# Parts of sums kept in DRAM instead of being built twice, in a float32 block of convolution and gated linear attention

## The chip, the cores and the metric

The kernel runs on one core of a Trainium2 chip (trn2). The metric is the time of one execution on the device in microseconds (us); the time of a kernel is the median of its runs. Beside it a profile of one execution shows what each engine did: TensorE (PE for matmuls, PEld for loading the stationary operand), VectorE (DVE), ScalarE (ACT), GpSimd (POOL) and SyncE (SP), which here does nothing but issue DMAs, in order.

## What is computed

One layer on 512 tokens of 2048 features, in float32. A combined projection feeds two branches, a short gated convolution and a chunked gated linear attention (GLA):

```python
h = rms_norm(x, norm_g)
ch, cb, cc, cz, gq, gk, gv, gr, gd = split(h @ w_in)      # 1024 x4, 512, 512, 1024, 1024, 16 columns
y_conv = cb * conv3(cc * ch) * silu(cz)                   # causal, three taps, per column
glog   = log_sigmoid(gd @ w_up + b_gate) / 16             # 8 chunks of 64 tokens
state  = exp(sum(glog over chunk)) * state + k_dec.T @ gv # per chunk, 4 heads
y_gla  = head_norm(gq @ state) * silu(gr)
out    = rms_norm(x + concat(y_conv, y_gla) @ w_out, final_g)
```

## The kernel before

**Numbers.** Each float32 operand is split into a high part (a cast to the matmul's own float32 form, on ScalarE) and a low part (the difference, on VectorE), and each product is three matmuls: high by high, low by high and high by low. `split_small` (lines 146 to 151) splits a tile of 128x512, `split` (124 to 126) one of 128x1024.

**Units with seven products.** The value columns, the four convolution groups and part of the output are done by `st_unit` (641 to 722): each of its five units before the output, named UV, 0, 1, 2 and 3, replaces the eight block products of a 2x2 split of both operands by seven, of 48 matmuls each. For this it needs sums of quarters of the activations, called s1, s2, s3 and s4: `sums` (552 to 566) makes four tiles of 128x512 for each of four pairs `j`, with one VectorE operation each (line 559). s4, s1 and s2 are then split into two parts each; s3 is kept whole, and `place_third` (598 to 601) splits it into the place of the second half of tokens of the normed activations `hT`. Sums of quarters of the weights are made on VectorE while the unit runs (line 687).

**The same sums, twice.** `quarter_sums(j)` (578 to 582) loads two 512 KB blocks of `xT` (tiles `raw_qx`), scales each half on ScalarE (line 574), makes the sums and splits them. It runs once for each `j` between the four `q_head` calls, for UV. During UV `restore_quarter` puts the normal second half of `hT` back for the eight `r_block` calls that come next, between which the steps of GLA run. The parts of the sums are given up after UV, because GLA needs the buffers. After `r_block(6)` come `quarter_sums(0)` and `(1)`, after `r_block(7)` `(2)` and `(3)`, a second time, for units 0 to 3; `place_third` then runs again.

**Order of the program.** The engines' and queues' orders are laid out ahead of time by a list planner that takes program order as priority and lets an instruction go early when its data and buffers are there. Buffers come from pools: `k2` has 44 tiles of 128x512, among them all parts of the sums; `raw` has 8 blocks of 128x1024 for loaded weights, for `raw_qx` and for the rows that go into `y_raw`; the high and low parts of weights have 4 blocks each. All loads and stores but ten stand on SP's queue. Eight of the ten are the copies of the chunk decays, 2 KB each, which ScalarE issues; four small transposes (`dp`, line 366) read them on TensorE.

**Already kept in DRAM.** `keep` is a pool in DRAM. `r_block` stores its result as `r_raw` (line 528), and `gated_rows` loads it back at the end of unit 0, multiplies it by `oT` and stores it as `y_raw` (lines 506 to 512).

Of the kernel before, what the change touches and what calls it, by code (L numbers as in the profile page):

```python
# [8 lines left out]
F32 = mybir.dt.float32  # L9
# [4 lines left out]
P = 128  # L14
D = 2048
S = 512
# [30 lines left out]
SPLITBUFS = 4  # L47
STC = 4
UV = 5
HT = S // 2  # L50


@with_exitstack
def hybrid_block(ctx: ExitStack, tc: tile.TileContext, xT, x, params, w_tm, w_ft, w_st, w_up, b_gate, w_out, final_g, out):
    nc = tc.nc
# [6 lines left out]
    keep = ctx.enter_context(tc.tile_pool(name="keep", bufs=1, space=bass.MemoryType.DRAM))  # L62
# [3 lines left out]
    def t2(name):  # L66
        return k2.tile([P, S], F32, tag="k2", name=name)

    def t2r(name):
        return k2.tile([P, S], F32R, tag="k2", name=name)  # L70
# [23 lines left out]
    for _ in range(WARM):  # L94
# [9 lines left out]
        out=trif[:, 0:P], in_=trif[:, 0:P], compare_op=ALU.is_gt, fill=0.0, base=0, pattern=[[-1, P]],  # L104
# [29 lines left out]
    def load_raw(src, n, name):  # L134
        raw = raw_tile(name)
        return raw, nc.sync.dma_start(out=raw[:, 0:n], in_=src)
# [9 lines left out]
    def split_small(t, name):  # L146
        hi = t2r(f"{name}_hi")
        lo = t2r(f"{name}_lo")
        nc.scalar.copy(out=hi, in_=t)
        nc.vector.tensor_sub(out=lo, in0=t, in1=hi.bitcast(F32))  # L150
        return hi, lo
# [11 lines left out]
    def load_x(kt):  # L163
        c, i = divmod(kt, HPC)
        if kt == 0:
            r = x_first
            nc.scalar.activation(hT_hi[c][:, i, 0:HT], r[:, 0:HT], AF.Copy, scale=g_in[:, 0:1])
            nc.vector.tensor_scalar(
                out=hT_hi[c][:, i, HT:S], in0=r[:, HT:S], scalar1=g_in[:, 0:1], scalar2=None, op0=ALU.mult
            )  # L170
# [120 lines left out]
    for tt in range(TT):  # L291
        nc.vector.tensor_scalar(
            out=dg[:, tt * P : (tt + 1) * P], in0=ident, scalar1=rstd[:, tt : tt + 1], scalar2=None, op0=ALU.mult
# [85 lines left out]
    def chunk_splits(tt):  # L379
        kv_split[tt] = [split_small(kv[tt][j], f"kv{tt}_{j}") for j in range(3)]  # L380
# [142 lines left out]
    def r_block(b):  # L523
        r = ft_unit(HEADS + b, b == 0)
        t1 = t2(f"r1_{b}")
        nc.vector.tensor_mul(out=t1, in0=r, in1=rB)
        nc.scalar.activation(t1, t1, AF.Silu)
        nc.sync.dma_start(out=r_raw[b], in_=t1)
# [17 lines left out]
    s_parts = {k: [None] * STC for k in (1, 2, 3, 4)}  # L546

    def quarters(a, b):
        av, bv = (r.rearrange("p (i t) -> p i t", i=2) for r in (a, b))
        return av[:, :, 0:HT], av[:, :, HT:S], bv[:, :, 0:HT], bv[:, :, HT:S]  # L550

    def sums(a, b, j, tag):
        a11, a21, a12, a22 = quarters(a, b)
        made = {}

        def put(k, op, in0, in1):
            made[k] = t2(f"{tag}{k}_{j}")
            v = made[k].rearrange("p (i t) -> p i t", i=2)
            nc.vector.tensor_tensor(out=v, in0=in0, in1=in1, op=op)
            return v  # L560

        v1 = put(1, ALU.add, a21, a22)
        v2 = put(2, ALU.subtract, v1, a11)
        put(4, ALU.subtract, a12, v2)
        put(3, ALU.subtract, a11, a21)
        return made

    def quarter_raws(j):
        raws = []
        for k0 in (2 * j, QK + 2 * j):  # L570
            raw, _ = load_raw(xT[:, k0 : k0 + 2, :], UNIT, f"qx{k0}")
            for i in range(2):
                sl = slice(i * S, (i + 1) * S)
                nc.scalar.activation(raw[:, sl], raw[:, sl], AF.Copy, scale=g_in[:, k0 + i : k0 + i + 1])
            raws.append(raw)
        return raws

    def quarter_sums(j):
        made = sums(*quarter_raws(j), j, "qs")
        for k in (4, 1, 2):  # L580
            s_parts[k][j] = split_small(made[k], f"qp{k}_{j}")
        s_parts[3][j] = made[3]


    def restore_quarter(j):
        raw = t2(f"rq{j}").rearrange("p (i t) -> p i t", i=2)
        nc.sync.dma_start(out=raw, in_=xT[:, 2 * j : 2 * j + 2, HT:S])
        for i in range(2):
            kt = 2 * j + i
            c, r = divmod(kt, HPC)  # L590
            nc.scalar.activation(hT_hi[c][:, r, HT:S], raw[:, i, :], AF.Copy, scale=g_in[:, kt : kt + 1])
            nc.vector.scalar_tensor_tensor(
                out=hT_lo[c][:, r, HT:S], in0=raw[:, i, :], scalar=g_in[:, kt : kt + 1],
                in1=hT_hi[c][:, r, HT:S].bitcast(F32), op0=ALU.mult, op1=ALU.subtract,
            )
# [29 lines left out]
    def product(ps, factor, name, c, w, first, last):  # L625
        wh, wl = w
        for r in range(2):
            i = 2 * c + r
            fs = [factor(name, i, t) for t in range(2)]
            sl = slice(r * S, (r + 1) * S)  # L630
            for k, (part_, ww) in enumerate(((0, wh), (1, wh), (0, wl))):
                for t in range(2):
                    nc.tensor.matmul(  # L633
                        ps[t], lhsT=fs[t][part_], rhs=ww[:, sl],
                        start=first and c == 0 and r == 0 and k == 0,
                        stop=last and c == STC - 1 and r == 1 and k == 2, skip_group_check=True,
                    )
# [3 lines left out]
    def st_unit(u, factor, out, before_out, into=None, between=()):  # L641
# [6 lines left out]
        def kept(ps, i, j):  # L648
            if into is not None:
                ts = [into(i, j, t) for t in range(2)]  # L650
                add(ts, ps)
                return ts
            ts = [t2(f"c{i}{j}_{u}_{t}") for t in range(2)]
            for t in range(2):
                nc.scalar.copy(out=ts[t], in_=ps[t])
            return ts
# [7 lines left out]
        c11 = kept(pa, 0, 0)  # L664
        if u in (0, UV):
            for j in range(STC):
# [16 lines left out]
        for c in range(STC):  # L683
# [23 lines left out]
            product(p7, factor, "s3", c, w3, True, True)  # L707
            if u == UV:
                restore_quarter(c)
# [50 lines left out]
    def ahead_of(u):  # L760
        def go():
            for c in range(2):
                st_weights(u, c, B11)

        return go
# [34 lines left out]
    for hh in range(HEADS):  # L800
        q_head(hh)
        quarter_sums(hh)
    ahead_of(UV)()
    st_unit(UV, h_factor, v_cols, next_rows)
    chunk_splits(0)
    for b in range(8):
        r_block(b)
        if b >= 6:
            for j in range(2):
                quarter_sums(2 * (b - 6) + j)  # L810
    for _ in steps:
        pass

# [205 lines left out]
    for c in W_ORDER[CH - 3 :]:  # L1019
        raw, _ = load_raw(w_out[3, c], UNIT, f"wl{c}")  # L1020
# [83 lines left out]
```

## Time and profile before

| what | value |
| --- | --- |
| time, median of 3 runs | 773.54 us (772.46 to 773.93) |
| time of the profiled execution | 774.64 us |
| its span, first to last instruction | 772.8 us |
| TensorE's mean granted clock | 0.997 of full speed |
| DMA, whole span | 151.94 MB, 197 GB/s on average |

Times within the profile count from the start of the span. A granted clock of 1.00 is 2.4 GHz. A matmul counts as busy until its modelled end, so neighbours overlap; what tells is whether TensorE had a gap, and who ended it. The stages follow one another on TensorE: the token-major projection to 51 us, `q_head` to 100, unit UV to 178, `r_block` and GLA to 286.57, unit 0 from there to about 362, then units 1, 2 and 3 to 597, and the output.

### The profile page before, as it was taken

The numbers are of one execution on the slowest core, as the hardware profiler recorded it, in microseconds if no ns is written. First come the engines' busy times: TensorE is split into PE (matmuls) and PEld (weight loads), VectorE is DVE, ScalarE is ACT, GpSimd is POOL, SyncE is SP. The second block draws the span as 40 slices with busy tenths as digits, with TensorE's granted clock in tenths as the row PEclk, the third lists the DMA queues.
The fourth block names the chain that finished last, engine by engine and source line by source line (L and its number), as shares of the span: only waits on it lengthen the run. The fifth ranks groups of instructions, "written<-read, shape, count | busy, mean of one in ns | idle before, by whom it ended". The sixth has DMA issues, their size and how long they took to land.

```text
span 772.8 us, 10177 instructions
## 1 busy us (share of the span) xinstructions
PE 760.3 (98%) x3704; PEld 638.2 (83%) x3704; DVE 619.0 (80%) x767; ACT 418.8 (54%) x635; POOL 31.5 (4%) x38
## 2 busy tenths in 40 slices
PE   9999999999999999999999999999999999999995
PEld 9998877887878888888788888888888888888885
DVE  6465699999676679998897799968987998997913
ACT  6956664554788777534443445345436345633504
POOL 1000000000001000000000000000000000004601
PEclk9999999999999999999999999999999999999998
DMA  9984468664322358769756466655565459568006
GB/s 307 359 276 134 137 203 275 218 220 145 99 84 94 93 161 315 247 204 308 277 193 195 160 213 221 192 191 194 171 209 162 147 189 359 176 214 301 3 0 218
DMA packets 51606, 151.94 MB, mean 197 GB/s; under 512 B 6066, under 2 KB 7858, under 8 KB 51556
## 3 DMA queue, kind: packets, MB, share of 16 engines
q1 hardware_dynamic: 51012, 151.12, 58.8%
q8 instruction: 29, 0.48, 0.2%
q10 hardware_dynamic: 544, 0.18, 0.1%
q14 instruction: 21, 0.17, 0.1%
HBM read 141.82 MB, written 9.44 MB: 196 GB/s over the span
## 4 chain that ended last, share of the span: by engine, by line
PE 50%; issue 0%; DVE 0%; ACT 0%; ACTq 0%; POOLq 0%; POOL 0%
PE pa L633 10%; PE pc L633 6%; PE pf L633 6%; PE pe L633 6%; PE pd L633 6%; PE pb L633 6%; PE po L155 3%; PE po L157 3%; PE po L156 3%; PE pd L774 0%; PE pd L776 0%; PE tu L774 0%; PE tg L776 0%; PE po_h L157 0%; PE po_h L156 0%
## 5 line engine op out<-in xcount | busy, mean ns | idle before, releaser
L125 ACT CAST hi_sq_t<-raw_sq 128x1024 fp32r<-128x1024 f32 x96 | 101.0, 1054 | 132.6 <-PE pf L633 26.8
L126 DVE TENSOR_TENSOR lo_sq_t<-raw_sq,hi_sq_t 128x1024 fp32r<-128x1024 f32 x96 | 117.3, 1231 | 20.7 <-ACT hi_sq_t L125 20.7
L687 DVE TENSOR_TENSOR raw_sq<-raw_sq,raw_sq 128x1024 f32<-128x1024 f32 x96 | 116.5, 1220 | 6.9 <-DMA raw_sq<-in_w_st 5.8
L125 ACT CAST hi_st<-raw_st 128x1024 fp32r<-128x1024 f32 x72 | 75.8, 1053 | 75.6 <-PE pb L633 24.0
L126 DVE TENSOR_TENSOR lo_st<-raw_st,hi_st 128x1024 fp32r<-128x1024 f32 x72 | 86.7, 1220 | 15.7 <-ACT hi_st L125 15.5
L155 PE MATMUL ft<-hhi,hi_ft 128*128 128x512 f32 x192 | 75.8, 395 | 0.0
L156 PE MATMUL ft<-hlo,hi_ft 128*128 128x512 f32 x192 | 75.1, 391 | 0.0
L157 PE MATMUL ft<-hhi,lo_ft 128*128 128x512 f32 x192 | 74.8, 390 | 0.0
L126 DVE TENSOR_TENSOR lo_ft<-raw_ft,hi_ft 128x1024 fp32r<-128x1024 f32 x24 | 29.2, 1222 | 17.9 <-ACT hi_ft L125 17.8
L155 PEld LDWEIGHTS ft<-hhi,hi_ft 128*128 128x128 f32 x192 | 36.1, 188 | 7.7
L157 PEld LDWEIGHTS ft<-hhi,lo_ft 128*128 128x128 f32 x192 | 36.1, 188 | 7.6
L156 PEld LDWEIGHTS ft<-hlo,hi_ft 128*128 128x128 f32 x192 | 36.1, 188 | 7.2
L918 POOL TENSOR_TENSOR res<-res,fg 128x512 f32<-128x512 f32 x12 | 21.8, 1844 | 438.2 <-DMA fg<-in_final_g 432.2
L155 PE MATMUL po<-hi_wo,yh 128*128 128x512 f32 (+1 forms) x104 | 39.6, 381 | 0.0
L156 PE MATMUL po<-lo_wo,yh 128*128 128x512 f32 (+1 forms) x104 | 39.5, 379 | 0.0
L157 PE MATMUL po<-hi_wo,yl 128*128 128x512 f32 (+1 forms) x104 | 39.1, 379 | 0.0
L265 PE MATMUL tm<-hi_tm,hhi 128*128 128x264 f32 x128 | 36.7, 287 | 0.0
L265 PE MATMUL tm<-hi_tm,hlo 128*128 128x264 f32 x128 | 36.4, 284 | 0.0
L265 PE MATMUL tm<-lo_tm,hhi 128*128 128x264 f32 x128 | 36.2, 284 | 0.0
L125 ACT CAST hi_ft<-raw_ft 128x1024 fp32r<-128x1024 f32 x24 | 25.0, 1050 | 12.5 <-PE ft L156 7.6
L633 PE MATMUL pa<-lo_st,hhi 128*128 128x512 f32 x80 | 25.1, 393 | 1.5 <-DVE lo_st L126 1.5
L633 PE MATMUL pd<-lo_sq_t,qp_hi 128*128 128x512 f32 x80 | 24.8, 391 | 0.5 <-DVE lo_sq_t L126 0.5
(287 smaller groups left out, 1797.5 us busy)
## 6 DMA issues: line engine op xcount, KB each, us to landing
raw_sq<-in_w_st SPq DMA_DIRECT2D x80, 512.0 KB, 4.3
raw_st<-in_w_st SPq DMA_DIRECT2D x60, 512.0 KB, 3.7
raw_ft<-in_w_ft SPq DMA_DIRECT2D x24, 512.0 KB, 4.3
raw_qx<-in_xT SPq DMA_DIRECT2D x16, 512.0 KB, 3.6
raw_sq<-in_w_out SPq DMA_DIRECT2D x16, 512.0 KB, 4.2
raw_wo<-in_w_out SPq DMA_DIRECT2D x13, 512.0 KB, 3.4
raw_st<-in_w_out SPq DMA_DIRECT2D x12, 512.0 KB, 7.7
rawx<-in_xT SPq DMA_DIRECT2D x16, 256.0 KB, 5.7
```

What stands on the lines that cost most here:

```text
L125: nc.scalar.copy(out=hi, in_=full)
L126: nc.vector.tensor_sub(out=lo, in0=full, in1=hi.bitcast(F32))
L155: nc.tensor.matmul(ps, lhsT=ah, rhs=bh, start=first, stop=False)
L156: nc.tensor.matmul(ps, lhsT=ah, rhs=bl, start=False, stop=False)
L157: nc.tensor.matmul(ps, lhsT=al, rhs=bh, start=False, stop=last)
L265: nc.tensor.matmul(tm_banks[b][tt][:, 0:TMC], lhsT=a[:, tt * P : (tt + 1) * P], rhs=wi, start=kt == 0 and k == 0, stop=kt == KT - 1 and k ...
L633: nc.tensor.matmul(ps[t], lhsT=fs[t][part_], rhs=ww[:, sl], start=first and c == 0 and r == 0 and k == 0, stop=last and c == STC - 1 and r ...
L687: nc.vector.tensor_tensor(out=dst, in0=x0, in1=x1, op=op)
L918: nc.gpsimd.tensor_mul(out=res[tt][cbk], in0=res[tt][cbk], in1=fg[cbk])
```

## The change

The parts that the first building makes are stored to DRAM as they appear: two of each of s4, s1 and s2 and the whole s3, seven tiles of 256 KB for each `j`, 28 in all. At the place of the second building the same seven tiles are loaded for each `j` into new buffers, and nothing is computed. Both stand on SP's queue. The first building, `place_third` and the units are as before.

```diff
+S_SLOTS = {4: 0, 1: 2, 2: 4}
...
+    s_keep = keep.tile([7 * STC, P, S], F32, name="s_keep")
+
+    def kept_sums(j):
+        for k in (4, 1, 2):
+            s_parts[k][j] = [t2r(f"qk{k}_{j}_{i}") for i in range(2)]
+            for i in range(2):
+                nc.sync.dma_start(out=s_parts[k][j][i].bitcast(F32), in_=s_keep[S_SLOTS[k] * STC + i * STC + j])
+        s_parts[3][j] = t2(f"qk3_{j}")
+        nc.sync.dma_start(out=s_parts[3][j], in_=s_keep[6 * STC + j])
+
     def quarter_sums(j):
         made = sums(*quarter_raws(j), j, "qs")
         for k in (4, 1, 2):
             s_parts[k][j] = split_small(made[k], f"qp{k}_{j}")
+            for i in range(2):
+                nc.sync.dma_start(out=s_keep[S_SLOTS[k] * STC + i * STC + j], in_=s_parts[k][j][i].bitcast(F32))
         s_parts[3][j] = made[3]
+        nc.sync.dma_start(out=s_keep[6 * STC + j], in_=made[3])
...
         if b >= 6:
             for j in range(2):
-                quarter_sums(2 * (b - 6) + j)
+                kept_sums(2 * (b - 6) + j)
```

## Rows read from the trace of the kernel before

**Rows 1.** The page: busy time of each engine, share of span, instructions.

```profile
PE 760.3 (98%) x3704; PEld 638.2 (83%) x3704; DVE 619.0 (80%) x767; ACT 418.8 (54%) x635; POOL 31.5 (4%) x38
```

**Rows 2.** TensorE's waits: line and releaser, total us, times, longest.

```profile
PE pa L633 <- DVE lo_st L126: 1.5, 1, 1.5
...
PE o L421 <- ACT oT L462: 0.9, 1, 0.9
PE pd L633 <- DVE lo_sq_t L126: 0.5, 1, 0.5
PE dp L366 <- DMA dec<-ke: 0.4, 1, 0.4
```

**Rows 3.** Windows: length; busy PE, PEld, DVE, ACT, POOL; clock, DMA share, GB/s.

```profile
250.00:300.00 50.00, 50.00 (x238) 41.84 (x237) 36.67 (x54) 37.48 (x75) 1.01 (x1) 1.00 0.49 160
300.00:350.00 50.00, 50.00 (x222) 41.42 (x221) 49.07 (x50) 25.34 (x29) 0.00 (x0) 1.00 0.74 247
```

**Rows 4.** Groups by line and form: count, busy us, mean ns, idle before.

```profile
L574 ACT ACTIVATE raw_qx<-raw_qx,par 128x512 f32<-128x512 f32 x32 | 22.4, 720 | 4.6 <-DMA raw_qx<-in_xT 4.6
...
L150 DVE TENSOR_TENSOR qp_lo<-qs,qp_hi 128x512 fp32r<-128x512 f32 x24 | 16.2, 685 | 0.8 <-ACT qp_hi L149 0.7
...
L149 ACT CAST qp_hi<-qs 128x512 fp32r<-128x512 f32 x24 | 14.3, 623 | 5.3 <-DVE qs L559 5.3
...
L559 DVE TENSOR_TENSOR qs<-raw_qx,raw_qx 128x512 f32<-128x512 f32 x8 | 5.5, 683 | 0.0
```

**Rows 5.** Timeline of SP's queue, 199 to 278 us: start, us, issue.

```profile
199.66 0.33 SPq L136 DMA_DIRECT2D raw_qx<-in_xT  x1
...
277.77 0.33 SPq L136 DMA_DIRECT2D raw_st<-in_w_st  x1
```

**Rows 6.** Timeline of ScalarE, 212 to 221 us.

```profile
212.53 1.33 ACT L574 ACTIVATE raw_qx<-raw_qx,par 128x512 f32<-128x512 f32 x2
...
220.00 1.12 ACT L462 ACTIVATE oT<-tp,par 128x128 f32<-128x128 f32 x4
```

**Rows 7.** Timeline of SP's queue, 353 to 373 us.

```profile
353.57 5.01 SPq L512 DMA_DIRECT2D y_raw<-raw_yg  x3
358.62 14.36 SPq L136 DMA_DIRECT2D raw_st<-in_w_st  x9
```

**Rows 8.** Timeline of VectorE, 370 to 376 us.

```profile
370.24 5.76 DVE L126 TENSOR_TENSOR lo_st<-raw_st,hi_st 128x1024 fp32r<-128x1024 f32 x5
```

**Rows 9.** DMA issues: count, KB each, median us to landing.

```profile
raw_sq<-in_w_st SPq DMA_DIRECT2D x80, 512.0 KB, 4.3
...
r_raw<-r SPq DMA_DIRECT2D x8, 256.0 KB, 2.1
```

**Rows 10.** Waits of SP's queue: total us, times, longest.

```profile
SPq L528 <- ACT r L527: 26.4, 8, 5.7
```

**Rows 11.** Windows, columns as in rows 3.

```profile
110.00:130.00 20.00, 20.00 (x92) 16.56 (x91) 19.39 (x28) 11.02 (x17) 0.00 (x0) 1.00 0.79 262
365.00:370.00 5.00, 5.00 (x23) 3.83 (x21) 5.00 (x9) 3.96 (x5) 0.00 (x0) 1.00 0.96 382
```

**Rows 12.** Timeline of SP's queue: the fourth of the first `raw_sq` loads.

```profile
122.73 0.33 SPq L136 DMA_DIRECT2D raw_sq<-in_w_st  x1
```

**Rows 13.** Timeline of VectorE, 127 to 135 us.

```profile
127.85 0.69 DVE L150 TENSOR_TENSOR qp_lo<-qs,qp_hi 128x512 fp32r<-128x512 f32 x1
...
130.44 3.49 DVE L687 TENSOR_TENSOR raw_sq<-raw_sq,raw_sq 128x1024 f32<-128x1024 f32 x3
133.84 1.22 DVE L126 TENSOR_TENSOR lo_sq_t<-raw_sq,hi_sq_t 128x1024 fp32r<-128x1024 f32 x1
```

**Rows 14.** Tile of the chunk decays: its DMAs.

```profile
DMA to landing us min/median/max: 3.0/3.8/4.7
```

**Rows 15.** Timeline of TensorE: the first matmuls of unit 0.

```profile
286.57 0.62 PE L633 MATMUL pa<-hi_st,hhi 128*128 128x512 f32 x2
```

**Rows 16.** Timeline of ScalarE: the first weight cast of unit 0.

```profile
281.66 1.06 ACT L125 CAST hi_st<-raw_st 128x1024 fp32r<-128x1024 f32 x1 [1.09 <-DMA raw_st<-in_w_st]
```

## Prediction

> **What bounds the kernel now.** I read the page's busy times first: TensorE is busy 760.3 of 772.8 us, VectorE 80% and ScalarE about half [rows 1]. So nothing that only frees VectorE or ScalarE can give more than TensorE loses by waiting. That loss is in the view of waits for TensorE: 1.5 us for a low weight part in the unit that starts near 362 us, 0.9 us for ScalarE's `oT` copies, 0.5 us for a low part in the value unit, 0.4 us for the DMA of the chunk decays [rows 2]. The four make 3.3 us, 0.4% of the run; what is left before the end (the warm-up, the last row blocks' scaling and stores) is touched by no step of this change. Next, the stretches where the removed work stands: from 250 to 350 us TensorE is busy 50.00 of 50.00 us twice, at a granted clock of 1.00 (2.4 GHz), while VectorE climbs from 36.67 to 49.07 [rows 3]. VectorE is nearly full there, and still nobody on TensorE waits for it.
>
> **Removed.** The second building of the sums: half of the groups of lines 574, 149, 150 and 559, whose counts are for both buildings [rows 4]. On ScalarE (22.4 + 14.3) / 2 = 18.4 us in 28 instructions. On VectorE 16.2 / 2 = 8.1 us of `qp_lo`, and four groups of 559, 8 instructions and 5.5 us each (one is shown), so 22.0 / 2 = 11.0 us: 19.1 us. Eight loads of 512 KB from `xT` go too, 4.2 MB. At the place where these run, 250 to 310 us, the gain is 0: TensorE's full 50.00 us [rows 3] is the cover, and VectorE's backlog is worked off while TensorE runs on blocks already split. Bounds: nothing below 0 lost, nothing above 0 won there, since TensorE waits for nothing in it.
>
> Two waits elsewhere could shrink. First, 0.9 us near 220 us for `oT`. The second building's `raw_qx` loads begin at 199.66 us [rows 5], 75 us before their sums, and ScalarE scales them early: two copies, 1.33 us, at 212.53, straight ahead of the split of `r`'s weights. ScalarE then gets to the last `oT` copies at 220.00 [rows 6], and TensorE's chunk outputs wait for the bank they empty. With 1.33 us of copies gone from that queue the wait can go whole: bounds 0 and -0.9. I take -0.9, because ScalarE is the engine named and the removed work stands in its queue within 8 us. Second, 1.5 us at 370 us. There SP stands on stores of `y_raw` from 353.57 to 358.62 before it issues the next weight loads [rows 7], and VectorE gives the late low part from 370.24 on [rows 8], after the sums of the unit that has just ended. The removed work ended 60 us earlier, and the stores wait for a product of `oT` and `r`, not for a sum. Bounds 0 and -1.5; I take 0.
>
> **Added: 28 stores of 256 KB** (7.3 MB) seven for each pair `j`, on SP's queue, from the first building's first split near 79 us to its last `qp_lo` at 127.85 [rows 13]. Nobody reads them for 140 us, so a store's own duration costs nothing; the nearest row is the store of `r_raw`, 2.1 us to landing [rows 9]. What costs is their place: SP works in order, so a store whose part isn't ready holds the weight loads behind it. The eight `r_raw` stores hold SP 26.4 us in all, 3.3 us each on average and 5.7 at worst [rows 10], and around them TensorE lost nothing [rows 3]. In the value unit the cover is thinner. VectorE is busy 19.39 of 20 us from 110 to 130 us while DMA moves 262 GB/s [rows 11]. That is 5.24 MB; the 14 stores of j = 2 and 3 add 3.67 MB, 8.91 MB together, and at the 382 GB/s of the fullest stretch shown [rows 11] this takes 23.3 us, 3.3 us more than there is. The loads with the least to spare are the first four `raw_sq`: the fourth is issued at 122.73 [rows 12] and lands a median 4.3 us later [rows 9], at 127.0; VectorE's first differences start at 130.44, the first low part at 133.84 [rows 13], and there TensorE already waits its 0.5 us. So the spare is 130.4 - 127.0 = 3.4 us. Bounds: 0 if one delay of 3.3 us comes (3.3 below 3.4); 3.3 + 3.3 - 3.4 = +3.2 us if the held queue and the full DMA engines add up. I take +0.5: that the wait there doubles, because the end at 0 is nearer to the `r_raw` row but VectorE, already full, has no time to catch up. What is late next would be every low part after it, by the same time, until the value unit ends.
>
> One wait is for a DMA on ScalarE's own queue, the eight 2 KB copies of the decays: TensorE stands 0.4 us on their transposes, and the value unit's matmuls are queued behind. They land in 3.0 to 4.7 us, in stretches where SP's queue is busy and where it isn't [rows 14]. The seven stores of j = 1 come just before, 1.84 MB, 4.8 us at 382 GB/s. Bounds 0 and the spread of the row, +1.7; I take 0. On this the Trainium skill, DMA: Bandwidth & Descriptors, section Queues, rings and completion order, says that each DMA engine takes turns between its queue rows packet by packet. By that rule the small copies don't stand behind the stores and the term is 0; were they behind all seven, it would be 4.8 us. The spread of only 1.7 us agrees with the rule so far.
>
> A part now keeps its buffer until its store is read. For the third sum, which is released early, this is some 3 us longer in one of 44 buffers; the others live to the end of the unit anyway. I take 0; its bound is the store's 3.3 us on SP, already in the 3.2 above.
>
> **Added: 28 loads of 256 KB** (7.3 MB, 19.2 us at 382 GB/s) in place of eight of 512 KB. They need only free buffers. These are handed out in program order: the sums of j = 0 and 1 had to come after `r_block(6)`'s tile near 275 us, so the loads too start near 275 us, and the others after `r_block(7)`, near 290. First needed are the parts of s4, by the third product of unit 0, 22 us after its first matmul at 286.57 [rows 15], so near 308 us: 14 loads need 9.6 us, so this is covered by 12 us and more. The unit's first weights gain: before, `raw_qx` took the raw buffers from 199.66 on and the first `raw_st` load of unit 0 had to wait to 277.77 [rows 5]; with those eight gone the weights follow `raw_ft` straight away. Bounds 0 and +3 (the second slow rival); I take 0.
>
> **Sum.** The profiled execution took 774.64 us, 772.8 of span and 1.84 around it. -0.9 + 0.5 = -0.4 makes a span of 772.4 and 774.2 in all. That execution is 1.1 us above the median of the runs shown, so against 773.54 the forecast is 773.1 us. A difference of 0.2% (1.55 us) is about what a measurement of this kernel can tell from no change, so this is no change.
>
> **Rivals.**
> Both ScalarE's wait and the one at 370 us go, and the stores are hidden: -0.9 - 1.5 = -2.4, 771.1 us. For it: both waits lie behind the early stretch that the change relieves, and the whole order on each engine is laid out anew. Against it: what holds SP at 358 us is a store that stays. With the 0.5 and the 0.4 as well it would be 770.2, the floor.
> The stores hold the value unit's weights: +3.2 from the two delays together, less 0.9, +2.3: 775.8 us. It decides from the point where the fourth `raw_sq` load lands after 130.4 us. For it: VectorE is full from 110 to 130 us, DMA would be asked for 445 GB/s. Against: the last part of j = 3 exists only after 127.85 [rows 13], so most of that pair's stores come behind these four loads.
> The loads hold unit 0's first weights: 14 reads ahead of the first `raw_st` load keep the DMA engines for 9.6 us from 275.6, to 285.2; with 1.4 us for its own 512 KB and a cast of 1.06 [rows 16] the first matmul could start at 287.7 instead of 286.57, and at 291 if the load also takes a landing of 4.3 us after them: +1.1 to +4.5. With a middle of 3: 773.1 + 3 = 776.1. Against: the raw buffers that these loads waited for are free 60 us earlier.
> That the change doesn't do what it says I give nothing: the second building's instructions are simply not issued.
>
> **Chances.** Forecast 0.46; both waits go 0.28; stores hold the value unit 0.18; loads hold unit 0 0.08. The forecast is a little below the old time, so a small part of it falls to faster: 0.30 faster, 0.44 within 0.2%, 0.26 slower. Range: from 770.9, just under the first rival, to 776.6, the stores' case with 0.8 us of the gain at 220 us gone too; the forecast's own range is 772.0 to 775.1.
>
> **What would show it.** Right: `raw_qx` with half its instructions, VectorE some 19 us and ScalarE 18 us less busy, all of it before 320 us; TensorE's busy time unchanged; the wait `o` on `oT` gone; the wait `pd` on the low part at 135 us near 1 us; the wait at 370 us still there; unit 0's first weight loads before 250 us. Wrong: a DMA as releaser of VectorE's differences near 130 us, SP waiting for `qp_lo` by more than 3 us at a time, a wait of TensorE at the start of unit 0, or a new order on SP near 345 us that frees the loads held at 358 us.

## The result and the profile after

The changed kernel takes 777.37 us (median of four runs, 777.3 to 777.63) where the kernel before takes 773.58 (772.46 to 773.93). The ratio is 1.0055, 95% interval 1.0042 to 1.0067: slower by about half a per cent, and above the range of the prediction. Its profiled execution took 777.3 us with a span of 775.4. Line numbers of the changed kernel and of the experiments are shifted by 1 to some 20 against those of before. In the lines, `pa` to `pf` are the sums that a unit's products add into, `raw_st` and `raw_sq` are loaded blocks of weights, and `hi_sq_t` and `lo_sq_t` are the high and the low part of a difference of two `raw_sq` blocks.

The removed work is gone, as the busy times on the page show (compare [rows 1]):

```profile
PE 760.6 (98%) x3704; PEld 638.7 (82%) x3704; DVE 603.3 (78%) x739; ACT 404.2 (52%) x607; POOL 32.0 (4%) x38
```

VectorE has 28 instructions and 15.7 us less, ScalarE 28 and 14.6 us, and TensorE's work is unchanged. The waits of TensorE show what that was worth, line and releaser first, then total us, times and longest (compare [rows 2]):

```profile
PE pd L647 <- ACT hi_sq_t L126: 3.4, 1, 3.4
PE dp L367 <- DMA dec<-ke: 1.3, 1, 1.3
...
PE pa L647 <- DVE lo_st L127: 0.2, 1, 0.2
```

Both waits that the removed work might have caused are gone or nearly so (`o` on `oT` from 0.9 to nothing, `pa` near 370 us from 1.5 to 0.2), but the value unit's two waits have grown, from 0.5 to 3.4 and from 0.4 to 1.3 us. Where the time went by stages is read from TensorE's timeline, as the starts of the first matmul of each stage:

| from, to | before, us | after, us | difference |
| --- | --- | --- | --- |
| start of the span to the value unit's first `pa` | 99.98 | 99.43 | -0.55 |
| to its first `pd` | 33.62 | 38.19 | +4.57 |
| to the first `ft` of `r_block` | 44.30 | 45.14 | +0.84 |
| to unit 0's first `pa` | 108.67 | 107.78 | -0.89 |
| to unit 1's first `pc` | 99.81 | 98.42 | -1.39 |

The sum is +2.58 us, and the spans differ by 2.6; behind the last row the two kernels run alike. So the value unit (second and third row) loses 5.4 us, and 2.3 us come back later. What the 0.55 us of the first row are isn't shown. That the medians differ by 3.8 and not 2.6 is the 1.1 us by which the profiled execution of before lay above its median.

The place of the loss, in TensorE's timeline of the changed kernel (start, duration, in brackets the idle time and its releaser):

```profile
133.56 0.61 PE L647 MATMUL pc<-lo_st,qp_hi 128*128 128x512 f32 x2
137.62 1.22 PE L647 MATMUL pd<-hi_sq_t,qp_hi 128*128 128x512 f32 x2 [3.44 <-ACT hi_sq_t L126]
138.64 1.05 PE L647 MATMUL pd<-hi_sq_t,qp_lo 128*128 128x512 f32 x2
139.50 1.05 PE L647 MATMUL pd<-lo_sq_t,qp_hi 128*128 128x512 f32 x2
140.35 0.84 PE L647 MATMUL pd<-hi_sq_t,qp_hi 128*128 128x512 f32 x2
141.03 0.63 PE L647 MATMUL pd<-hi_sq_t,qp_lo 128*128 128x512 f32 x2
```

Pairs of matmuls follow one another every 0.45 us before the gap. The four pairs behind it take 141.03 - 137.62 = 3.41 us instead of 1.82, so the gap is followed by a loss of another 1.6 us. The windows (columns as in [rows 3]) give the granted clock for this, a mean of 0.74 of 2.4 GHz in the stretch of the gap's end:

```profile
125.00:130.00 5.00, 5.00 (x24) 4.14 (x23) 5.00 (x7) 2.99 (x6) 0.00 (x0) 1.00 0.94 328
130.00:135.00 5.00, 4.18 (x19) 3.13 (x17) 0.97 (x3) 0.96 (x2) 0.00 (x0) 1.00 0.99 330
135.00:140.00 5.00, 2.38 (x6) 1.90 (x7) 3.59 (x4) 1.17 (x3) 0.00 (x0) 0.74 1.02 384
```

From 130 to 135 us VectorE is busy 0.97 of 5 us: it isn't late, it is starved. Its timeline and ScalarE's name a DMA (compare [rows 13], where the differences start at 130.44):

```profile
135.27 1.23 DVE L701 TENSOR_TENSOR raw_sq<-raw_sq,raw_sq 128x1024 f32<-128x1024 f32 x1 [4.29 <-DMA raw_sq<-in_w_st]
...
136.53 1.04 ACT L126 CAST hi_sq_t<-raw_sq 128x1024 fp32r<-128x1024 f32 x1 [1.41 <-DVE raw_sq L701]
```

And SP's timeline says why the DMA was late (compare [rows 12]):

```profile
112.06 0.33 SPq L596 DMA_DIRECT2D s_keep<-qs  x1
...
117.11 1.40 SPq L137 DMA_DIRECT2D raw_st<-in_w_st  x3
122.81 0.33 SPq L596 DMA_DIRECT2D s_keep<-qs  x1
...
125.96 0.45 SPq L137 DMA_DIRECT2D raw_sq<-in_w_st  x1
127.27 0.32 SPq L594 DMA_DIRECT2D s_keep<-qp_lo  x1
...
129.01 0.32 SPq L594 DMA_DIRECT2D s_keep<-qp_lo  x1
129.38 1.77 SPq L137 DMA_DIRECT2D raw_sq<-in_w_st  x3
```

The planner put all seven stores of j = 2 and four of j = 3 ahead of the first `raw_sq` load, and the last three of j = 3 ahead of the second. VectorE's first difference needs the first two of these loads. The second was issued at 118.10 us before:

```profile
118.10 0.33 SPq L136 DMA_DIRECT2D raw_sq<-in_w_st  x1
```

Now it is issued at 129.38 and lands 5.8 us later instead of 4.3, at 135.2, where the difference starts. The fourth load, on which the prediction's sum went, is issued near 131 us instead of 122.73. The eight loads issued from 110 to 140 us land a median 8.3 us after their issue, where 4.5 was the median before. The queue stood on the stores: in SP's view of waits for 75 to 150 us the stores of `qp_lo` hold it 6.2 us in nine waits, and those of `qs` 8.3 us in two.

At the other end everything is as wanted: unit 0's first weights are issued at 219.90, the kept parts are loaded from 278.40 to 298.9, and TensorE has no gap in the 100 us around them (compare [rows 3]):

```profile
250.00:300.00 50.00, 50.00 (x253) 41.75 (x252) 24.60 (x35) 30.00 (x65) 2.02 (x2) 1.00 0.56 192
300.00:350.00 50.00, 50.00 (x222) 41.38 (x222) 43.62 (x41) 22.73 (x26) 0.00 (x0) 1.00 0.75 264
```

### The profile page after: what moved, and what is told of

It is laid out like the page before. It is cut to its first block, busy times and chain, and to the rows that moved or that the text cites. A ratio compares the mean times of both kernels' runs of the same rounds, so it can differ in the third digit from the quotient of the medians.

```text
span 775.4 us, 10207 instructions
## 1 busy us (share of the span) xinstructions
PE 760.6 (98%) x3704; PEld 638.7 (82%) x3704; DVE 603.3 (78%) x739; ACT 404.2 (52%) x607; POOL 32.0 (4%) x38
## 4 chain that ended last, share of the span: by engine, by line
PE 87%; DVE 5%; DMA 3%; issue 2%; ACT 1%; ACTq 0%; SPq 0%; POOLq 0%; POOL 0%; DVEq 0%
PE pa L647 15%; PE pd L647 8%; PE pf L647 7%; PE pe L647 7%; PE pc L647 7%; PE pb L647 7%; PE tm L266 6%; PE ft L157 5%; PE ft L156 5%; PE ft L158 5%; PE po L157 3%; PE po L156 3%; PE po L158 3%; DVE lo_sq_t L127 1%; DVE raw_sq L701 1%
## 5 line engine op out<-in xcount | busy, mean ns | idle before, releaser
L647 PE MATMUL pc<-hi_st,qk 128*128 128x512 f32 x128 | 34.8, 391 | 0.0
L647 PE MATMUL pd<-hi_sq_t,qk 128*128 128x512 f32 x128 | 34.2, 389 | 0.0
L647 PE MATMUL pa<-hi_sq_t,qk 128*128 128x512 f32 x128 | 34.2, 389 | 0.0
```

The source lines that it names most:

```text
L647: nc.tensor.matmul(ps[t], lhsT=fs[t][part_], rhs=ww[:, sl], start=first and c == 0 and r == 0 and k == 0, stop=last and c == STC - 1 and r ...
```

## Experiments

The theory: the stores, by their place on SP's queue ahead of the weight loads and by their bytes, delay `raw_sq`; the rest of the change gains a little. The rivals: the loads or the missing second building do the harm; or the place alone, or the bytes alone. A profile shows one execution, which can lie some us from its kernel's median. Of each kernel the median, its runs, and the ratio to the kernel before in the same batch of runs (773.26, 773.24 and 772.98 us there, 22 to 24 runs each):

| kernel | us | runs | ratio, 95% interval |
| --- | --- | --- | --- |
| loads without stores | 771.81 | 7 | 0.9979, 0.9967 to 0.999 |
| stores without loads, second building kept | 778.67 | 4 | 1.0068, 1.0053 to 1.0083 |
| stores on GpSimd's queue | 775.38 | 10 | 1.0023, 1.0012 to 1.0034 |
| stores of 16 of 512 columns | 774.94 | 10 | 1.0019, 1.0008 to 1.003 |
| stores of pairs 1 to 3 late | 770.83 | 10 | 0.9973, 0.9964 to 0.9982 |
| first pair kept alone | 775.84 | 9 | 1.0034, 1.0022 to 1.0046 |
| whole sums kept, split twice | 775.61 | 10 | 1.0029, 1.0018 to 1.004 |
| pairs 2 and 3 late | 773.19 | 11 | 1.0002, 0.999 to 1.0014 |
| pair 1 late | 775.43 | 6 | 1.003, 1.0019 to 1.0041 |
| late stores, second building kept | 771.69 | 12 | 0.9986, 0.9977 to 0.9995 |

**1. Loads without stores.**

```diff
-                nc.sync.dma_start(out=..., in_=s_keep[S_SLOTS[k] * STC + i * STC + j])
+                nc.sync.dma_start(out=..., in_=s_one)
...
-            for i in range(2):
-                nc.sync.dma_start(out=s_keep[...], in_=s_parts[k][j][i].bitcast(F32))
+            if j == 0 and k == 4:
+                nc.sync.dma_start(out=s_one, in_=s_parts[k][j][0].bitcast(F32))
```

> Of the change only the loads: at the place of the second building 28 loads of 256 KB, all from one stored part (so the conv units get wrong sums; 27 of the 28 stores are left out). If the stores do all the harm and the removed building all the good, the value unit's wait of 3.4 us is back to at most 0.5 us, both gains (near 220 and 370 us) stay, and the time is 773.6 - 0.9 - 1.3 = 771.4 us. If the loads themselves or the new order cost something, 773 us or more. Rival that the gain near 370 us came only from TensorE running late: 772.7 us.

771.81 us. TensorE's wait for `pd` is back at 0.5 us, the waits at 220 and 370 us are gone; its plan has a new wait of 1.6 us near 85 us. The loads do no harm.

```profile
PE pd L646 <- DVE lo_sq_t L127: 0.5, 1, 0.5
```

**2. Stores without loads.**

```diff
-                kept_sums(2 * (b - 6) + j)
+                quarter_sums(2 * (b - 6) + j, False)   # builds again, stores nothing
```

> Of the change only the stores: the 28 stores stand in the first building, nothing is read back, the second building stays. If the stores do the harm: the value unit loses the same 5.4 us (waits of TensorE 3.4 and 1.3 us and the lower clock behind them), no gain elsewhere, 773.6 + 5 = 778 to 779 us. If the harm needs the loads or a longer hold of buffers after the value unit: 773.6 us.

778.67 us (777.37 in the profile), and both waits of the value unit are there:

```profile
PE pd L648 <- ACT hi_sq_t L126: 2.5, 1, 2.5
PE dp L367 <- DMA dec<-ke: 1.6, 1, 1.6
```

The harm is that of the stores alone. The waits for `oT` and near 370 us are gone here too, though the second building stays.

**3. The same stores on another queue.**

```diff
-                nc.sync.dma_start(out=s_keep[...], in_=...)
+                nc.gpsimd.dma_start(out=s_keep[...], in_=...)
```

> The whole change, with the 28 stores issued from GpSimd's queue and not from SP's: the same bytes at about the same time, but no weight load stands behind a store in the same queue. Theory A (the stores' place in SP's order makes the loads late): the wait of 3.4 us in the value unit falls below 1 us and the time is 771 to 772.5 us. Theory B (14.7 MB more through the DMA engines make them late): the wait stays above 2.5 us and the time is 776 to 777.5 us.

775.38 us, between the kernel before and the changed one; the profile is of the fastest of the ten executions, 773.26 us. The `raw_sq` loads are issued early again, from 117.45 us with no store between them, but those issued from 110 to 140 us land a median 6.4 us after their issue, with the DMA engines full (windows):

```profile
120.00:125.00 5.00, 5.00 (x24) 4.14 (x23) 4.89 (x8) 2.24 (x4) 0.00 (x0) 1.00 1.03 420
```

What is left of the waits is 1.3 us for `pd` and 2.2 us for `dp`. So the bytes cost without the place, but less, as far as one profile tells: held up by `dp`, TensorE comes to `pd` at 135.29 us instead of 133.60, which gives the loads more time.

**4. The same stores in SP's queue, with few bytes.**

```diff
-                nc.sync.dma_start(out=s_keep[...], in_=s_parts[k][j][i].bitcast(F32))
+                nc.sync.dma_start(out=s_keep[...][:, 0:16], in_=s_parts[k][j][i][:, 0:16].bitcast(F32))
```

> The whole change, with each of the 28 stores cut to 16 of 512 columns (8 KB of 256 KB) in the same place on SP's queue, plus one whole store, from which all 28 loads read (the conv units get wrong sums). The waits on SP for parts stay, the bytes go. Theory A (place in SP's order): the value unit still loses 3 us or more, 775.5 to 777.4 us. Theory B (bytes): the loss is gone, 771.4 to 772.5 us.

774.94 us. There is no wait for `pd`. The planner put three `raw_sq` loads ahead of pair 3 here and the fourth at 128.12 us, so the queue is held less than in the changed kernel, and after the `dp` wait TensorE comes to `pd` only at 135.13 us. The test of the place alone is not clean. What is left stands elsewhere in the waits, at `dp`, and at 370 us although nothing is built a second time:

```profile
PE dp L367 <- DMA dec<-ke: 2.4, 1, 2.4
PE pa L650 <- DVE lo_st L127: 1.4, 1, 1.4
```

**5. Stores of pairs 1, 2 and 3 behind the `raw_sq` loads of the value unit.**

```diff
-            b11, b12, b21, b22 = (load_raw(...)[0] for q in range(4))
+            loads = [load_raw(st_source(u, c, q), UNIT, f"sq{u}_{c}_{q}") for q in range(4)]
+            b11, b12, b21, b22 = (ld[0] for ld in loads)
+            if u == UV and c < STC - 1:
+                with tc.issue_after(loads[-1][1].ins):
+                    store_sums(c + 1)
```

`store_sums(j)` issues the seven stores of pair j; in the first building it now stands for j = 0 alone.

> The whole change with the same 28 stores on SP's queue, but only those of the first pair at their old place: those of pairs 1, 2 and 3 are put behind the loads of the weights that the unit's second half needs first, second and third. If the loss came from stores standing ahead of these weight loads and moving their bytes beside them, the wait on the first differences (3.4 us) falls to the old 0.5, the wait for the chunk decays (1.3) to the old 0.4, and the time is 771.4 to 772.6 us. If the bytes hurt wherever they fall in this unit, the wait only moves some 10 to 20 us on and the time stays above 775 us.

770.83 us, below the changed kernel by 6.5 us and below the kernel before by about 2.4. SP's timeline shows the new order, the four loads in front and pair 1's seven stores behind them:

```profile
114.97 7.29 SPq L137 DMA_DIRECT2D raw_sq<-in_w_st  x4
122.31 0.42 SPq L592 DMA_DIRECT2D s_keep<-qp_hi  x1
...
126.74 0.95 SPq L593 DMA_DIRECT2D s_keep<-qs  x1
127.78 2.26 SPq L137 DMA_DIRECT2D raw_sq<-in_w_st  x3
```

VectorE's differences follow its other work without a gap at 129.64 us, and TensorE waits for nothing in the whole span but the 1.1 us of the warm-up. The same bytes are stored in the same unit; they only come after the loads. From 125 to 160 us the DMA engines are as busy as in experiment 3 (a share of 1.02, 372 GB/s), and TensorE is busy all of the 35 us:

```profile
125.00:130.00 5.00, 5.00 (x24) 4.14 (x23) 5.00 (x9) 0.81 (x2) 0.00 (x0) 1.00 1.02 389
```

Not all that is won here comes from the stores' new place. The wait of 0.5 us for `pd`, which the kernel before has too, is gone, and the planner lays two differences ahead of the first low part on VectorE where there were three ([rows 13], x3):

```profile
129.64 2.47 DVE L710 TENSOR_TENSOR raw_sq<-raw_sq,raw_sq 128x1024 f32<-128x1024 f32 x2
```

The profiles with three have that wait (before, 1, 6 and 8, and 3, where it is longer), those with two (4, 5, 7 and 10) don't.

**6. The first pair alone is stored and loaded; the others are built twice.**

```diff
-                kept_sums(2 * (b - 6) + j)
+                if b == 6 and j == 0:
+                    kept_sums(0)
+                else:
+                    quarter_sums(2 * (b - 6) + j, False)
```

> Of the change only the first pair: seven stores near 80 us, where the DMA engines are a third busy, seven loads; pairs 1 to 3 are built a second time as before. If only the later stores hurt, the value unit's waits are those of the kernel before (0.4 and 0.5 us). The scale copies of the first pair, which stood on ScalarE near 206 and 213 us, are gone, so the wait for oT near 220 us (0.9 us) goes: 772.4 to 773.0 us. If these copies had nothing to do with that wait: 773.3 us.

775.84 us, a miss. The wait for `oT` stays at 0.9 us. The next pair's scaling took the place of the first one's on ScalarE, with the same number of copies, at 211.50 us (compare the first line of [rows 6]):

```profile
211.50 1.33 ACT L575 ACTIVATE raw_qx<-raw_qx,par 128x512 f32<-128x512 f32 x2
```

The profile was of the fastest of the nine executions, 774.14 us, and no wait in it is 2.6 us longer than before. Some 0.4 of the 2.6 us lie outside the span, which is 2.2 us shorter than the time in all nine executions, against 1.8 to 1.9 before. Another profile of it:

> The kernel that keeps the first pair alone, profiled once more. Its first profile is of the fastest of nine executions (774.1 against a median of 775.8, up to 777.7) and has no dp wait. Theory: slower executions of it lose up to 3.5 us at the decays' transposes, so a profile at 775.8 us or more shows a dp wait of 1 us or more with a lower granted clock near 112 us. Rival: the slower executions lose their time elsewhere, then the dp wait stays at 0.5 us or less and another wait is new or longer. If the profile falls near 774 us again, the two are not told apart.

This one took 776.89 us and has no `dp` wait; the rival holds. Its view of waits has a new one, at the start of unit 1, absent from the first profile:

```profile
PE pa L652 <- DVE c L679: 1.8, 1, 1.8
```

VectorE, busy 5.00 of 5 us there, comes to the last combinations of unit 0 too late. 776.89 - 774.14 = 2.75 us, of which the new wait is 1.8. Why it comes in one execution and not in another stays open.

**7. The four whole sums are stored, 16 tiles in place of 28, and split a second time.**

```diff
-            for i in range(2):
-                nc.sync.dma_start(out=s_keep[...], in_=s_parts[k][j][i].bitcast(F32))
+            nc.sync.dma_start(out=s_keep[k * STC + j], in_=made[k])
...
+            s_parts[k][j] = split_small(t, f"qk{k}_{j}")
```

> Instead of the parts the whole sums are stored and loaded, 16 tiles instead of 28 (4.2 instead of 7.3 MB each way), and s4, s1 and s2 are split a second time. The stores don't wait for splits and take 57% of the bytes. If the loss is the sum of SP's order and the bytes, each smaller here, the wait on the first differences lies between 0.5 and 1.5 us, too short to lower the clock, and the time is 772 to 774 us.

775.61 us, a miss. The value unit is as in the kernel before (33.50 and 43.52 us in the table's second and third rows), but TensorE now waits four times in unit 0 between 314 and 329 us, once for a part of a stored sum (0.6 us), then for the high part of a weight (1.1), for a low part (0.9) and for ScalarE's copy of a result (1.0), at a granted clock of 0.84 and 0.82 from 320 to 325 and from 325 to 330 us. The table's last row becomes 104.38 us. The second split, which the change had taken away, now stands on ScalarE and VectorE among the parts that are late; that it makes them late is not shown by a run of its own. The expectation's waits "too short to lower the clock" do not hold either: two gaps of 1.1 and 0.9 us, 1.2 us apart, were followed by matmul pairs every 0.85 us.

**8 and 9. Late stores for some pairs only.** In the first, pairs 0 and 1 are stored as in the change and 2 and 3 late; in the second, pair 1 alone is late. Against experiment 5:

```diff
-        if j == 0:
+        if j < 2:          # 8; in 9: if j != 1
             store_sums(j)
...
-            if u == UV and c < STC - 1:
+            if u == UV and 0 < c < STC - 1:    # 8; in 9: c == 0
```

> The stores of pairs 0 and 1 stand where the change has them; those of pairs 2 and 3 come behind the second and third set of raw_sq loads. Theory: the value unit's 3.4 us wait is made by pairs 2 and 3 standing ahead of the first raw_sq loads, the decays' wait by pair 1's bytes on the DMA engines. Then the pd wait is 0.5 us or less with the clock at 1.00 after it, the dp wait stays at 1 to 1.5 us, and the time is that of the kernel with three late pairs (770.8) plus about 1: 771.4 to 772.4 us. Rival: any store in the value unit before 135 us brings the long wait, then 774 us or more. Second rival: the decays are late for another reason than pair 1's stores, then no dp wait and 770.8.

> The stores of pair 1 come behind the first set of raw_sq loads; those of pairs 2 and 3 stand where the change has them. Theory: pairs 2 and 3 alone make the value unit's wait, so pd 2.5 to 3.5 us with the lower granted clock after it, the decays' wait gone, and a time of 775.5 to 777 us, about 1 us below the changed kernel. Rival: the harm is the sum of three pairs' bytes before 130 us, so that leaving one out takes away more than a third of it: pd under 1.5 us and 773 us or less.

Pairs 2 and 3 late: 773.19 us, scattered from 771.62 to 776.76; the profiled execution, 775.39 us, has the `pd` wait at 0.5 us, as the theory has it, and a `dp` wait of 2.3, longer than the 1 to 1.5 us of the theory, with a granted clock of 0.66 behind it. The median is 0.8 us above what was expected. Pair 1 late: 775.43 us, a hair under the expected range, with no `dp` wait and the long one at the unit's next product; the clock is granted at 0.70 from 140 to 145 us:

```profile
PE pe L652 <- ACT hi_sq_t L126: 2.7, 1, 2.7
```

So pairs 2 and 3 make the long wait, and that of the decays goes with the early stores of pair 1. The landings of the eight decay copies say the same. Their longest is 5.0 to 6.6 us in the five kernels that store seven tiles of pair 1 early (the changed one and 2, 3, 4 and 8), but 3.3 to 4.7 in the kernel before and in all others. As the view of the tile gives it for the changed kernel and, second, for pair 1 late:

```profile
DMA to landing us min/median/max: 1.7/2.9/5.0
```

```profile
DMA to landing us min/median/max: 1.7/1.8/3.4
```

It is not the bytes of these stores alone: the longest landing of all, 6.6 us, is that of experiment 4, whose stores are 8 KB each. What goes with the landings is how busy the DMA engines are from 105 to 110 us, while the last four copies are under way: 0.92 to 1.04 in the five kernels, 0.35 to 0.37 where the longest landing is 3.3 or 3.4, and 0.56 to 0.83 where it is 4.0 to 4.7. For the changed kernel, experiment 4 and pair 1 late, in this order (columns as in [rows 3]):

```profile
105.00:110.00 5.00, 3.88 (x18) 2.88 (x16) 3.00 (x6) 2.81 (x4) 0.00 (x0) 1.00 0.97 352
```

```profile
105.00:110.00 5.00, 3.94 (x18) 2.94 (x16) 3.06 (x6) 2.52 (x4) 0.00 (x0) 1.00 0.92 277
```

```profile
105.00:110.00 5.00, 5.00 (x26) 3.92 (x25) 3.74 (x9) 2.61 (x4) 0.00 (x0) 1.00 0.37 107
```

In the changed kernel and in 2, 4 and 8 SP's queue holds `raw_st` loads behind the last stores of pair 1 until some 103 us, so that these loads run beside the copies; in 3 SP holds none back, but there the stores themselves, on GpSimd's queue, land a median 6.6 to 8.8 us after their issue.

**10. Late stores, and the second building kept; nothing is loaded.** The edit is that of 2 on top of that of 5.

> The late stores as in the kernel that was 770.8 us, but the sums are built a second time as before and nothing is loaded; the stored parts are read by nobody. Theory: late stores cost nothing and the gain of that kernel is the removed second building (the waits at 220 and 370 us), so this one is back at the kernel before: 772.8 to 773.8 us, with the o wait near 0.9 us and the pa wait near 370 us there again. Rival: the gain comes from the new order that the planner makes of it, or from an earlier start of r_block, then 771 to 772 us without those waits.

771.69 us, the rival's time: 1.1 us faster than before by the ratio, with the whole building still there. The `oT` wait is absent although ScalarE still scales the blocks around 214 us. So a good part of what 5 wins is the order that the planner makes, not the removed work. The profiled execution is the slowest of the twelve, 774.7 us, and shows a wait for the decays with no store of pair 1 ahead of them:

```profile
108.70 0.39 PE L652 MATMUL pa<-lo_st,hhi 128*128 128x512 f32 x1
110.97 0.38 PE L367 MATMUL dp<-ident,dec 8*128 8x8 f32 x4 [1.88 <-DMA dec<-ke]
...
112.27 1.06 PE L652 MATMUL pa<-hi_st,hlo 128*128 128x512 f32 x2
113.12 1.06 PE L652 MATMUL pa<-lo_st,hhi 128*128 128x512 f32 x2
```

> The kernel with late stores and the second building, profiled once more. Its first profile is of the slowest of twelve executions (774.7 against a median of 771.7) and has a wait of 1.9 us of the decays' transposes dp, with no store ahead of them. Theory: that wait comes and goes between executions of one kernel, and with the lower granted clock behind it it is worth about 3 us. Then a profile near 771.7 us has no dp wait over 0.5 us, and one near 774.7 has it. Rival: the scatter lies elsewhere, so a profile near 771.7 has the dp wait too, or one near 774.7 lacks it.

The second profile took 771.66 us and has no `dp` wait: as the theory said. The gap of 1.9 us and the matmul pairs at 0.85 us in place of 0.45 behind it, at a granted clock of 0.68 from 110 to 115 us, which cost another 1.5, make the value unit 3.5 us longer; the wait near 370 us, some 0.8 shorter in that execution, brings the difference down to 3.0. In the slower execution ScalarE had stood 3.61 us for a weight load up to 97.13 us and issued the last four decay copies at 104.76 instead of 103.56. So a `dp` wait of this size also comes without pair 1's stores, and one profile of 8 and one of 9 don't prove that they make it. The wait near 370 us is 0.2 in the slower execution and 1.0 in the other; that for `oT` is in neither.

## Why the prediction was wrong

**The step that failed** is the term of the stores, "I take +0.5: that the wait there doubles, because the end at 0 is nearer to the `r_raw` row". The value unit lost 5.4 us (4.57 + 0.84 in the table). 0.97 of it lie ahead of the first `pc`, where the decays' wait stands; the other 4.4 (3.60 from there to the first `pd` and 0.84 behind it) are the stores' term, above its own upper bound of 3.2. With the 2.8 us that the other rows won this makes +2.6, where the prediction had -0.4. Three things were wrong.

First the choice between the ends. It rested on the argument that the last part of j = 3 exists only after 127.85, so that "most of that pair's stores come behind these four loads". A planner that takes program order as priority does the opposite: the stores come first in the program, so the loads wait for them. The row that the prediction called nearest, the `r_raw` stores that hold SP and cost nothing, comes from a stretch in which the raw buffers are loaded far ahead. The gap grew from 0.45 to 3.44 us, by 3.0, close to the upper bound of 3.2 that it had worked out and not taken; but that the sum 3.3 + 3.3 - 3.4 comes so near is luck. VectorE waited for the second `raw_sq` load, not for the fourth, and this load had a spare of 130.44 - 122.4 = 8.0 us. Its issue came 11.3 us later, its landing took 1.5 longer, and 11.3 + 1.5 - 8.0 = 4.8 is the delay of the first difference, from 130.44 to 135.27. So most of the delay is the load's place on SP's queue. Experiment 5 shows that no wait is left when the loads go first, with the DMA engines just as busy, and 9 that pairs 2 and 3 are enough for the long wait. 3, the bytes without the place, still has 1.3 us of it, and 4, the place without the bytes, none; neither is a clean test.

Second, the bound held the gap alone, not what came with it: the loss of 1.6 us at the lower clock behind it. Third, the decays, a term of their own, costed at 0 with a bound of +1.7: their wait grew by 0.9 us. The prediction leaned there on the Trainium skill, DMA: Bandwidth & Descriptors, section Queues, rings and completion order, by which the engines take turns between queue rows packet by packet. Taking turns is not being undisturbed: the longest landing went from 4.7 to 5.0 us, and by experiments 8 and 9 landings and wait go with pair 1's stores and with how full the DMA engines are. The runs don't show how the packets were served. The row that the prediction read had a sign of this: in the kernel before, the copies issued up to 95 us landed after 3.0 to 3.1 us, the last four, beside more traffic, after a median of 4.1.

**Removed work, gain 0 in its place**: right. TensorE's 50.00 of 50.00 us from 250 to 300 and from 300 to 350 stand as before. The sizes on the other engines were some 20 to 25% too high (19.1 and 18.4 us forecast, 15.7 and 14.6 measured). Durations in the profile overlap, so that a count times a duration is more than the time it takes: the `qp_lo` of [rows 13] starts at 127.85 us and is 0.69 us long, and VectorE's next instruction starts at 128.45.

**The wait for `oT`, -0.9**: the wait went, but the reason given isn't shown. In experiment 6 a copy pair of the next pair's took the place of the first one's and the wait stayed, which fits; in 2 and in 10 the building stays whole and the wait is gone, which doesn't. So the removed work isn't needed for it; what in the planner's order is, stays open.

**The wait near 370 us, 0 of -1.5**: wrong, it fell to 0.2. The reason for leaving it was sound all the same: it isn't the removed work's. It goes in 2 and nearly in one profile of 10 with the building kept, and stays at 1.4 us in 4 and 1.1 in 8 with the building removed.

**Loads, 0**: right. Experiment 1 has the loads and is faster than before; unit 0's weights were issued at 219.90, as foreseen before 250. **Buffers held longer, 0**: no wait of TensorE names it, and no run tests it alone.

**The rivals.** What happened is the second, stores that hold the value unit's weights (0.18), with 4.4 in place of its 3.2, 1.0 more for the decays and 2.8 won elsewhere in place of its 0.9. Of its two marks one was met, a DMA as releaser of VectorE's differences; the other, SP waiting over 3 us at a time for `qp_lo`, was not: the longest for `qp_lo` is 0.9 us, and the long one of a store, 4.2 us, is for `qs`, the sum before its split. The first rival's two waits went as well, together 2.2 us; without the stores' harm it would have been the outcome (771.1 forecast, 771.81 in experiment 1 and 770.83 in 5).

What stays open: how much of the 2.4 us that experiment 5 wins is the removed building's. Between 10, which builds a second time, and 5, which loads in its place, lie 0.9 us, but their intervals meet. And why single executions of one kernel lose 1.9 us for a wait that others don't have is shown only as far as the late weight load in 10; the same scatter limits every reading here that rests on one profile.

## What to carry to other kernels

A store that nobody awaits still costs what is queued behind it: on a queue that issues in order, look at which loads the planner lets it overtake, and tie it behind them. For the price of a stall, go by the load that is needed first and by what the queue puts ahead of it, rather than by a middle between two bounds, and add what a lower clock can take after the gap. Work removed where TensorE never waits is worth little by itself: of the 15.7 us less on VectorE some 0.9 us came back, if that.

## What the runs showed of the hardware

The granted clock does not follow the length of a gap alone. After `dp` gaps of 2.2 and 2.4 us in experiments 3 and 4 it stayed at 1.00; after 1.9 and 2.3 us in 10 and 8 it was 0.68 and 0.66 from 110 to 115 us; after 2.7 us in 9 and 3.4 us in the changed kernel 0.70 and 0.74 in a stretch of 5 us. In 7 it fell behind gaps of 1.1 and 0.9 us that stood 1.2 us apart. Behind each of these the matmul pairs came every 0.85 in place of 0.45 us, at 0.50 of 2.4 GHz (from 113.0 to 114.8 us in 10), which is the lower of the two levels, 1.2 GHz; the mean of a stretch lies between. So a gap of about 2 us cost either itself alone or, as in 8 and 10, another 1.5 us.

SP's queue alone moved 413 GB/s from 140 to 145 us in experiment 9, more than the 382 that the prediction took from the fullest stretch shown; with the stores on GpSimd's queue, in 3, it was 420 from 120 to 125 us. The stores on GpSimd's queue then landed 6.3 to 8.7 us after their issue (medians by tile), against 2.6 to 3.5 on SP's.
